# One encoder layer for two groups: the queries' rotation by one product and transfers inside SBUF

## The chip, the cores and the metric

One core of one Trainium2 chip. The metric is the device time of one execution in microseconds; lower is better. Five engines work beside each other, each with its own queue that runs in order: TensorE (PE; its weight loads are shown as PEld), VectorE (DVE), ScalarE (ACT), GpSimd (POOL) and SyncE (SP), which issues most transfers. 16 DMA engines move the data.

## The reference, cut to what matters

One layer of a bidirectional encoder is applied to two groups ("prompt" and "sample") of 512 tokens, 1024 channels, with shared weights: norm, an input projection, an mLSTM branch and a latent attention branch, gates that merge them, an output projection, a SwiGLU block, a gated embedding, a last norm. The change is in the attention branch, in the rotation of the queries:

```python
def rope(x, cos, sin):
    x1, x2 = jnp.split(x, 2, axis=-1)
    return jnp.concatenate([x1 * cos - x2 * sin, x1 * sin + x2 * cos], axis=-1)

qa = (rmsnorm(c_q, g_q) @ w_uq).reshape(B, S, A_HEADS, A_NOPE + A_ROPE)
q_nope = qa[..., :A_NOPE]                       # 128 channels
q_rope = rope(qa[..., A_NOPE:], cos, sin)       # 64 channels, x1 and x2 of 32 each
k_rope = rope(k_r, cos, sin)                    # one key of 64 channels for all heads
s = q_nope @ k_nope.T + q_rope @ k_rope.T       # for each of 8 heads
p = softmax(s * scale)
o = p @ v
```

## The kernel before, in words

Activations lie transposed, channels on the 128 partitions and the 512 tokens of a group along the free axis, so a tile is 128x512 in fp32. Matmuls get about fp32 precision from three products of operands split into a high and a low part (ScalarE casts the high part, VectorE subtracts it from the source to get the low one).

The stages in order: input projections and mLSTM; some merge gates (`merge_gate`: a projection by TensorE, a product by VectorE, a tanh, a store through a tile of the tag "bk"); the values of all heads, stored to DRAM through tiles of the tags "ch" and "bk" in turn (lines 703 and 704, 16 tiles `av`); attention; then the merge, the output projection, the SwiGLU block and the rest as long chains of matmuls.

Attention runs over 8 heads, and for each over the 2 groups g. `attn_proj(hd, g)` prepares head hd: for even heads it makes the rotated queries of two heads at once (2 x 64 = 128 rows), then the query and key tiles (`qn`, `kn`), and loads the head's values (`avt`). All three projections go through one PSUM bank, tag "pj", of which there is one. `attn(hd, g)` makes the scores in four blocks, softmax, transposes and the product with the values; its output `oz` is copied into a tile of the tag "ch" and stored. In the program, head hd+1's projections of a group follow head hd's attention of that group.

`rope(src, nblk)` (lines 711 to 722) rotates nblk blocks of 32 rows. For the queries nblk is 4 and `src` is the bank "pj"; it is called 8 times, for heads 0, 2, 4, 6 and two groups. These are called the first to the eighth rotation here; they begin at 568.1, 581.3, 643.9, 669.3, 723.9, 747.1, 791.9 and 809.4 us. For the key nblk is 2. Line 714 makes the product with the cosines for all rows. Line 718 makes the product with the sines block by block and writes each to its neighbour block's rows of a scratch tile `rs` (blocks 0 and 1 change places, 2 and 3 too; the sign is in the table). Line 721 adds. Scratch `rs`, result `rp` and the loaded values `avt` share the tag "tr", which has three buffers. Behind the rotation, lines 744 to 747 split the result into high and low parts for the two heads.

Two things set the order around the change. A tile pool gives out the buffers of a tag in turn, in the order of the program, and a tile's first writer waits until the last user of the buffer's tile before is done, a store's transfer among them; the tag "ch" has two buffers. And the order on each engine's queue is not the program's: a planner simulates the kernel with its own durations and lays each queue out by the times at which it finds the instructions ready. Only stretches marked as pinned keep the program's order; the attention stage is not among them.

Of the kernel before, what the change touches and what calls it, by code (L numbers as in the profile page):

```python
# [11 lines left out]
ALU = mybir.AluOpType  # L12
# [50 lines left out]
def encoder_kernel(ctx: ExitStack, tc: tile.TileContext, a):  # L63
    nc = tc.nc
# [20 lines left out]
    V, S, E, GP = (Engine(e) for e in (nc.vector, nc.scalar, nc.tensor, nc.gpsimd))  # L85
# [23 lines left out]
    EV = Slots("EV", ch=2, bk=2)  # L109
# [249 lines left out]
    for g in range(G):  # L359
        s = EV("ch", "gsb")  # L360
# [25 lines left out]
    for d in range(2):  # L386
        st = R("tr", "mst")
        nc.sync.dma_start(st[:, 0:P], a["mask"][d])
        m = MC.pool.tile([P, P], F32R, name=f"mask{d}")
# [50 lines left out]
    for i in range(NB):  # L440
        c = slice(i * P, (i + 1) * P)
        V.tensor_tensor_scan(
            out=M[:, c], data0=A[0][:, c], data1=A[0][:, c], initial=mprev[:, i : i + 1], op0=ALU.max, op1=ALU.max
# [4 lines left out]
    for d in range(1, NB):  # L448
        GP.tensor_copy(out=A[d][:, (NB - d) * P : T], in_=A[0][:, (NB - d) * P : T])
        for j in range(NB - d):  # L450
            e = (j + d) * P - 1
            V.tensor_scalar(
                out=A[d][:, j * P : (j + 1) * P],
                in0=A[d - 1][:, j * P : (j + 1) * P],
# [12 lines left out]
    for d in range(NB + 1):  # L467
        src = A[d] if d < NB else em
# [239 lines left out]
    sin = Q.pool.tile([P, T], F32, name="sin")  # L708
    nc.sync.dma_start(sin, a["sin"])

    def rope(src, nblk):
        n = 32 * nblk
        r = Q("tr", "rp")
        V.tensor_tensor(out=r[0:n], in0=src[0:n], in1=cos[0:n], op=ALU.mult)
        s = Q("tr", "rs")
        for i in range(nblk):
            o = i ^ 1
            V.tensor_tensor(
                out=s[32 * o : 32 * o + 32], in0=src[32 * i : 32 * i + 32], in1=sin[32 * i : 32 * i + 32], op=ALU.mult
            )  # L720
        V.tensor_tensor(out=r[0:n], in0=r[0:n], in1=s[0:n], op=ALU.add)
        return r

    kst = []
    for g in range(G):
        gs = Q("tr", "gs")
        nc.sync.dma_start(gs[0:64], gsd[g])
        r = rope(gs, 2)
        kh = Q.pool.tile([P, T], F32R, name=f"kh{g}")
        kl = Q.pool.tile([P, T], F32R, name=f"kl{g}")  # L730
        for o in (0, 64):
            S.copy(kh[o : o + 64], r[0:64])
        for o in (0, 64):
            V.tensor_tensor(out=kl[o : o + 64], in0=r[0:64], in1=kh[0:64].bitcast(F32), op=ALU.subtract)
        kst.append((kh, kl))
# [3 lines left out]
    def attn_proj(hd, g, wa):  # L739
        if hd % 2 == 0:  # L740
            r = rope(proj1(wa, lat["cq"][g], 2, 0, "pj"), 4)
            st0 = Q("qst", "qs0", F32R)
            st1 = Q("qst", "qs1", F32R)
            S.copy(st0[0:64], r[0:64])
            S.copy(st1[64:128], r[64:128])
            V.tensor_tensor(out=st0[64:128], in0=r[0:64], in1=st0[0:64].bitcast(F32), op=ALU.subtract)
            V.tensor_tensor(out=st1[0:64], in0=r[64:128], in1=st1[64:128].bitcast(F32), op=ALU.subtract)
            qst[g] = [st0, st1]
        qn = split(proj1(wa, lat["cq"][g], 2, 256, "pj"), Q, "qkv", "qn")
        kn = split(proj1(wa, lat["ckv"][g], 2, 512, "pj"), Q, "qkv", "kn")  # L750
        vt = Q("tr", "avt")
        c = hd % 4 * P
        nc.sync.dma_start(vt.rearrange("p (a b) -> p a b", a=NB), vd[g][hd // 4].rearrange("a p c -> p a c")[:, :, c : c + P])
        vn = split(vt, Q, "qkv", "vn", GP)
        return qn, kn, vn, qst[g][hd % 2]
# [699 lines left out]
```

## Time and profile before

| | |
|---|---|
| time, median of 3 runs | 1897.68 us (1896.53 to 1899.62) |
| profiled execution | 1901.48 us, of which the span 1899.3 us |
| TensorE busy | 1849.6 us, 97% |
| VectorE busy | 1232.7 us, 65% |
| ScalarE busy | 881.6 us, 46% |
| GpSimd busy | 457.4 us, 24% |
| mean granted TensorE clock | 0.991 |

The span runs from the first to the last instruction of the profiled execution. Matmuls are pipelined and the profile models their ends, so a busy TensorE is one that has work under way, not one at its peak. Line numbers (L718) are those of the kernel before; a line can be that of a helper. "PEclk" is the clock that TensorE was granted, as a share of 2.4 GHz.

### The profile page before, as it was taken

The numbers are of one execution on the slowest core, as the hardware profiler recorded it, in microseconds if no ns is written. First come the engines' busy times: TensorE is split into PE (matmuls) and PEld (weight loads), VectorE is DVE, ScalarE is ACT, GpSimd is POOL, SyncE is SP. The second block draws the span as 40 slices with busy tenths as digits, with TensorE's granted clock in tenths as the row PEclk, the third lists the DMA queues.
The fourth block names the chain that finished last, engine by engine and source line by source line (L and its number), as shares of the span: only waits on it lengthen the run. The fifth ranks groups of instructions, "written<-read, shape, count | busy, mean of one in ns | idle before, by whom it ended". The sixth has DMA issues, their size and how long they took to land.

```text
span 1899.3 us, 24534 instructions
## 1 busy us (share of the span) xinstructions
PE 1849.6 (97%) x8849; PEld 1536.6 (81%) x8849; DVE 1232.7 (65%) x2158; ACT 881.6 (46%) x1717; POOL 457.4 (24%) x326
## 2 busy tenths in 40 slices
PE   9999999999999998999999998999999999999997
PEld 6888898988888877777877887888888887887886
DVE  6747575836555567885897586444444458878757
ACT  6255555534444565774534354333333344433432
POOL 1000000100000000332350035666466643322100
PEclk9999999999999999999999999999999999999998
DMA  4111111112253124345555241232323346534232
GB/s 164 51 45 35 56 34 66 36 56 73 84 187 121 53 70 119 95 150 197 164 189 185 94 164 56 89 133 92 103 90 111 112 148 226 164 127 135 88 122 89
DMA packets 98314, 207.60 MB, mean 109 GB/s; under 512 B 10704, under 2 KB 21328, under 8 KB 98192
## 3 DMA queue, kind: packets, MB, share of 16 engines
q1 hardware_dynamic: 86096, 163.03, 25.8%
q10 hardware_dynamic: 12096, 43.00, 7.0%
q8 instruction: 70, 1.15, 0.2%
q14 instruction: 52, 0.43, 0.1%
HBM read 151.89 MB, written 54.10 MB: 108 GB/s over the span
## 4 chain that ended last, share of the span: by engine, by line
PE 84%; DVE 10%; ACT 2%; DMA 2%; issue 2%; SPq 0%; DVEq 0%; ACTq 0%
PE b L917 12%; PE b L919 12%; PE b L918 12%; PE mm L183 8%; PE mm L185 8%; PE mm L184 8%; PE mm L79 3%; PE nm L603 3%; DVE xl L154 2%; PE mm L518 2%; PE mm L520 2%; PE mm L519 2%; DVE wp L154 1%; PE mm L1265 1%; PE mm L1266 1%
## 5 line engine op out<-in xcount | busy, mean ns | idle before, releaser
L919 PE MATMUL b<-xh,wp 128*128 128x512 f32 x1148 | 445.1, 393 | 7.4 <-DVE wp L154 7.4
L917 PE MATMUL b<-xh,wp 128*128 128x512 f32 x1148 | 442.3, 394 | 10.0 <-ACT wp L866 4.5
L918 PE MATMUL b<-xl,wp 128*128 128x512 f32 x1148 | 448.9, 392 | 0.0
L866 ACT CAST wp<-wst 128x512 fp32r<-128x512 f32 (+1 forms) x270 | 164.2, 612 | 309.9 <-PE b L919 264.4
L154 DVE TENSOR_TENSOR wp<-wst,wp 128x512 fp32r<-128x512 f32 (+1 forms) x270 | 240.8, 893 | 76.5 <-ACT wp L866 76.0
L917 PEld LDWEIGHTS b<-xh,wp 128*128 128x128 f32 x1148 | 216.6, 189 | 63.6 <-ACT wp L866 9.1
L919 PEld LDWEIGHTS b<-xh,wp 128*128 128x128 f32 x1148 | 216.4, 188 | 55.9 <-DVE wp L154 8.8
L918 PEld LDWEIGHTS b<-xl,wp 128*128 128x128 f32 x1148 | 216.3, 188 | 46.6
L183 PE MATMUL mm<-hh,whi 128*128 128x512 f32 x560 | 219.4, 392 | 0.0
L184 PE MATMUL mm<-hl,whi 128*128 128x512 f32 x560 | 219.3, 392 | 0.0
L185 PE MATMUL mm<-hh,wlo 128*128 128x512 f32 x560 | 218.9, 393 | 0.0
L892 POOL TENSOR_TENSOR s<-wst,wst 128x512 f32<-128x512 f32 (+1 forms) x42 | 67.2, 1600 | 425.0 <-DMA wst<-w 270.1
L957 DVE TENSOR_TENSOR u<-b,u 128x512 f32<-128x512 f32 x90 | 61.6, 689 | 143.8 <-PE b L919 87.4
L183 PEld LDWEIGHTS mm<-hh,whi 128*128 128x128 f32 x560 | 105.6, 188 | 22.0 <-DVE va L526 0.3
L184 PEld LDWEIGHTS mm<-hl,whi 128*128 128x128 f32 x560 | 105.6, 189 | 21.8
L185 PEld LDWEIGHTS mm<-hh,wlo 128*128 128x128 f32 x560 | 105.5, 188 | 21.8
L168 ACT CAST whi<-wst 128x1024 fp32r<-128x1024 f32 (+1 forms) x69 | 71.0, 1028 | 104.3 <-PE mm L184 61.8
L952 ACT COPY u<-b 128x512 f32<-128x512 f32 x90 | 50.9, 589 | 107.4 <-PE b L919 80.0
L154 DVE TENSOR_TENSOR xl<-ld,xh 128x512 fp32r<-128x512 f32 x121 | 92.3, 793 | 12.3 <-ACT xh L1199 6.5
L154 DVE TENSOR_TENSOR wlo<-wst,whi 128x1024 fp32r<-128x1024 f32 (+1 forms) x69 | 83.6, 1212 | 23.2 <-ACT whi L168 23.0
L154 POOL TENSOR_TENSOR vnl<-avt,vnh 128x512 fp32r<-128x512 f32 x16 | 21.4, 1339 | 306.2 <-ACT vnh L158 283.5
L895 POOL TENSOR_TENSOR wst<-wst,wst 128x512 f32<-128x512 f32 (+1 forms) x42 | 79.1, 1884 | 38.0 <-DVE wp L154 28.6
(348 smaller groups left out, 3632.7 us busy)
## 6 DMA issues: line engine op xcount, KB each, us to landing
wst<-w SPq DMA_DIRECT2D x74, 512.0 KB
wst<-w ACTq DMA_DIRECT2D x60, 512.0 KB
ld<-actd SPq DMA_DIRECT2D x77, 256.0 KB
actd<-t SPq DMA_DIRECT2D x44, 256.0 KB
actd<-sg SPq DMA_DIRECT2D x33, 256.0 KB
x<-x SPq DMA_DIRECT2D x32, 256.0 KB
ld<-hzd SPq DMA_DIRECT2D x32, 256.0 KB
wst<-wd ACTq DMA_DIRECT2D x16, 512.0 KB
```

The costliest lines, as they stand in the source:

```text
L154: e.tensor_tensor(out=out, in0=src, in1=hi.bitcast(F32), op=ALU.subtract)
L168: S.copy(hi[:, :n], st[:, :n])
L183: E.matmul(bk, whi[:, c], hi, start=k == 0, stop=False)
L184: E.matmul(bk, whi[:, c], lo, start=False, stop=False)
L185: last_mm[0] = E.matmul(bk, wlo[:, c], hi, start=False, stop=k == nk - 1)
L866: S.copy(hi, src)
L892: GP.tensor_tensor(out=src, in0=a11, in1=a21, op=ALU.add)
L895: GP.tensor_tensor(out=a11, in0=a11, in1=a21, op=ALU.add)
L917: E.matmul(bk, whi[:, c], hi, start=bool(first) and k == 0, stop=False, **sk)
L918: E.matmul(bk, whi[:, c], lo, start=False, stop=False, **sk)
L919: E.matmul(bk, wlo[:, c], hi, start=False, stop=k == self.kh - 1, **sk)
L957: V.tensor_tensor(out=t, in0=b, in1=t, op=ALU.add if name == "P2" else ALU.subtract)
```

## The change

For the rotations of four blocks, the products with the sines become one product of all 128 rows into a new tile `rm` of the tag "ch", and four transfers on SyncE's queue, each of 32 rows (64 KB), copy its blocks into the neighbour block's rows of the scratch tile. The addition that follows is as before. The key's rotation (two blocks) is as before.

```diff
         s = Q("tr", "rs")
+        m = EV("ch", "rm") if nblk == 4 else None
+        if m is not None:
+            V.tensor_tensor(out=m, in0=src, in1=sin, op=ALU.mult)
         for i in range(nblk):
-            o = i ^ 1
-            V.tensor_tensor(
-                out=s[32 * o : 32 * o + 32], in0=src[32 * i : 32 * i + 32], in1=sin[32 * i : 32 * i + 32], op=ALU.mult
-            )
+            f, o = slice(32 * i, 32 * i + 32), slice(32 * (i ^ 1), 32 * (i ^ 1) + 32)
+            if m is not None:
+                nc.sync.dma_start(s[o], m[f])
+            else:
+                V.tensor_tensor(out=s[o], in0=src[f], in1=sin[f], op=ALU.mult)
         V.tensor_tensor(out=r[0:n], in0=r[0:n], in1=s[0:n], op=ALU.add)
```

## Rows read from the trace of the kernel before

**Rows 1.** The page: span and busy time of each engine.

```profile
span 1899.3 us, 24534 instructions
...
PE 1849.6 (97%) x8849; PEld 1536.6 (81%) x8849; DVE 1232.7 (65%) x2158; ACT 881.6 (46%) x1717; POOL 457.4 (24%) x326
```

**Rows 2.** Busy time by stretch; its first line names the columns.

```profile
core 0: us, PE busy (x) PEld busy (x) DVE busy (x) ACT busy (x) POOL busy (x), PEclk, DMA share, GB/s
565.00:600.00 35.00, 35.00 (x160) 29.00 (x159) 22.96 (x36) 17.25 (x31) 2.24 (x2) 1.00 0.45 147
640.00:680.00 40.00, 38.34 (x182) 30.70 (x181) 29.62 (x63) 24.53 (x50) 2.58 (x2) 1.00 0.23 75
...
720.00:760.00 40.00, 34.33 (x156) 27.35 (x155) 32.99 (x65) 24.78 (x50) 2.69 (x3) 0.94 0.40 114
760.00:800.00 40.00, 36.74 (x177) 28.95 (x175) 36.76 (x73) 31.72 (x67) 13.56 (x10) 0.97 0.37 113
800.00:835.00 35.00, 33.09 (x160) 26.82 (x161) 26.75 (x60) 25.03 (x53) 5.13 (x4) 1.00 0.12 38
```

**Rows 3.** The chain of waits, 640 to 835 us: shares by line.

```profile
by line: PE pt L782 6.3%; PE mm L183 5.5%; PE mm L184 5.4%; PE mm L185 5.4%; PE pj L183 4.9%; DVE rs L718 4.7%; PE pj L184 4.5%; PE pj L185 4.5%; PE av L789 4.0%; PE av L790 3.9%; PE av L791 3.9%; DMA ld<-hzd 3.7%; PE sc L765 3.4%; PE sc L7
```

**Rows 4.** Line 718: count, min/median/max ns, first and last start.

```profile
L718 DVE TENSOR_TENSOR rs<-pj,sin x32: 680/686/697, 568.8 to 812.2; 32x512 f32<-32x512 f32 x32
```

**Rows 5.** Line 714, the same view: all 128 rows.

```profile
L714 DVE TENSOR_TENSOR rp<-pj,cos x8: 667/681/692, 568.1 to 809.4; 128x512 f32<-128x512 f32 x8
```

**Rows 6.** TensorE's waits, 560 to 835 us: total us, times, longest.

```profile
PE pj L183 <- DVE rs L718: 2.8, 2, 1.7
```

**Rows 7.** VectorE in time order, fourth rotation: start, us, instruction.

```profile
670.01 2.79 DVE L718 TENSOR_TENSOR rs<-pj,sin 32x512 f32<-32x512 f32 x4
...
675.56 0.68 DVE L721 TENSOR_TENSOR rp<-rp,rs 128x512 f32<-128x512 f32 x1
```

**Rows 8.** VectorE in time order, sixth, seventh and eighth rotation.

```profile
747.83 2.79 DVE L718 TENSOR_TENSOR rs<-pj,sin 32x512 f32<-32x512 f32 x4
...
754.25 0.69 DVE L721 TENSOR_TENSOR rp<-rp,rs 128x512 f32<-128x512 f32 x1
...
792.56 2.79 DVE L718 TENSOR_TENSOR rs<-pj,sin 32x512 f32<-32x512 f32 x4
...
796.18 0.68 DVE L721 TENSOR_TENSOR rp<-rp,rs 128x512 f32<-128x512 f32 x1
...
810.06 2.79 DVE L718 TENSOR_TENSOR rs<-pj,sin 32x512 f32<-32x512 f32 x4
...
814.88 0.68 DVE L721 TENSOR_TENSOR rp<-rp,rs 128x512 f32<-128x512 f32 x1
```

**Rows 9.** SyncE's queue in time order: small transfers issued early on.

```profile
51.46 0.36 SPq L400 DMA_DIRECT2D lf<-rid  x1
...
60.49 0.62 SPq L420 DMA_DIRECT2D rfn<-lfd  x2
```

**Rows 10.** VectorE: the first instruction behind each [idle before it].

```profile
53.25 0.23 DVE L401 SCALAR_TENSOR_TENSOR u<-lf 128x64 f32<-128x64 f32 x1 [4.10 <-DMA lf<-rid]
...
63.77 0.42 DVE L423 COPY rf<-rfn 32x512 f32<-32x512 f32 x1 [3.73 <-DMA rfn<-lfd]
```

**Rows 11.** Load of the key's rows: SyncE's queue, then VectorE.

```profile
541.95 0.46 SPq L727 DMA_DIRECT2D gs<-gsd  x1
...
546.67 0.68 DVE L714 TENSOR_TENSOR rp<-gs,cos 64x512 f32<-64x512 f32 x1 [0.99 <-DMA gs<-gsd]
```

**Rows 12.** SyncE's queue: stores of value tiles.

```profile
555.67 2.48 SPq L704 DMA_DIRECT2D vd<-av  x3
...
572.84 0.32 SPq L704 DMA_DIRECT2D vd<-av  x1
```

**Rows 13.** ScalarE in time order: the fifth value tile is written.

```profile
560.19 0.59 ACT L703 COPY av<-mm 128x512 f32<-128x512 f32 x1 [0.98 <-DMA vd<-av]
```

**Rows 14.** The chain of waits, 740 to 815 us, one of the longest pieces.

```profile
737.51 2.61 DMA tad<-tg
```

## The prediction

> **What bounds the kernel now.** I read the page first, then busy time by stretch, then the chain of waits over the stage that holds the rotations, then the single rotations in order of time. On the page TensorE is busy for 97% of the span [rows 1]; a change to VectorE can pay only where TensorE stands idle for it, so the question is which stretch that is. The eight rotations of queries begin between 568 and 809 us [rows 5]. By stretch [rows 2], TensorE is busy for the whole of 565 to 600 us, where the first two lie. From 640 to 680 it loses 1.7 us, from 720 to 760 5.7, from 760 to 800 3.3, from 800 to 835 1.9. In those same stretches VectorE is busy 74%, 82%, 92% and 76% of the time, and from 760 to 800 ScalarE, at 79%, is the next. So the late part of attention is set by VectorE and the early part by TensorE. The chain of waits agrees: of 640 to 835 us, line 718 (the sine products) has 4.7%, which is 9.2 us, the largest share of any VectorE line that the row shows [rows 3]. Six rotations lie in that span, with 6 x 2.79 = 16.7 us of sine products; a little over half of it is on the chain. TensorE waits twice, 2.8 us in all, straight for the sine product that releases its single pj bank [rows 6].
>
> **The change part by part.**
>
> *Three products go.* A product of 32 rows takes 686 ns [rows 4], one of all 128 rows out of the same bank 681 ns [rows 5]. Four become one: 3 x 0.69 = 2.07 us of VectorE less per rotation, 16.6 us in eight. What is on the path: the first and second lie where TensorE is dense [rows 2], and I count them at nothing; so I do with the third and fifth, as the 9.2 us of sine products on the chain are no more than some three to four rotations of 2.79. The work that hides these four is TensorE's own dense sequence. If that cover were gone each would give up to 2.07. The fourth, sixth, seventh and eighth (products at 670.0, 747.8, 792.6 and 810.1 us [rows 7, 8]) lie in stretches bound by VectorE: 4 x 2.07 = 8.3 us. The 2.8 us of waits for the bank are within this, as the bank comes free 2.07 us sooner.
>
> *Four transfers come.* They wait for the product, and the addition (line 721) waits for them on VectorE's queue, which runs in order; whatever is queued behind the addition waits too, and ScalarE's casts and TensorE's transposes for that. No row shows a transfer from SBUF to SBUF. The nearest: two small loads issued together at 60.49 us let VectorE go on at 63.77, 3.3 us later; one, issued at 51.46, at 53.25, 1.8 us later [rows 9, 10]. With other traffic about, the 128 KB of the key rows took from 541.95 to 546.67, 4.7 us [rows 11], and a value tile's store, issued at 555.67, held the next writer of its buffer until 560.19, 4.5 us [rows 12, 13]. An issue costs 0.31 us (two in 0.62), so the fourth goes out 0.93 us after the first. The rows therefore put the scratch between 0.93 + 1.8 = 2.7 and 0.93 + 4.7 = 5.6 us behind the product; the pair is the row most like it, and with two more issues gives 3.3 + 0.62 = 3.9 us, which I take.
>
> What covers 3.9 us? Between the end of the first product and the addition there were 4.9, 5.7, 2.9 and 4.1 us in the four rotations that count [rows 7, 8]; without the three products 2.8, 3.7, 0.9 and 2.1 us of other VectorE work are left, 9.4 in all. With this work alone the additions would stand for 1.1 + 0.2 + 3.0 + 1.8 = 6.1 us (3.9 less each), and of the 8.3 us only 2.2 would be left. But the order of the queue is written anew, and the planner puts other instructions ahead of one that waits for a transfer. How well it does this is shown by the key rows: its plan left 0.99 us of idle time behind the transfer [rows 11]. I take 1.0 us per rotation, 4.0 us, and keep 6.1 for the range. The queries' own way to the scores gets some 2 us longer; I cost that at nothing after the first head, as the rotation of two heads on is issued well ahead of its scores; if that lead is gone, it is 2 us per rotation.
>
> *SyncE.* 32 issues x 0.31 = 9.9 us of a queue that mostly waits. Behind a transfer that waits for its product stand loads of value tiles, weights and stores. I take nothing; the bound is one rotation's four issues, 1.2 us, for each of the four loads behind them that VectorE or ScalarE waits for, 5 us.
>
> *Buffers.* The product goes to the two-buffer "ch" tag, and that is new. The first rotation's product takes the buffer of the thirteenth value tile, whose store is issued at 572.84 [rows 12]; at 2.6 us (a store on the chain [rows 14]) to 4.5 us [rows 13] it is free at 575.4 to 577.3, 6.6 to 8.5 us after the sine products began at 568.8 [rows 4]. The pj bank is held for as long, and with it the head's two other projections. TensorE has the rest of the values and the merge gates to run, so I take 1.0 us, with bounds of 0 and 8.5. Later products wait for the store of an attention output; in the seventh rotation that store comes a few microseconds after the place where the product is now, and I cost the slide at nothing, with a bound of 3. The three-buffer scratch tag holds its tile 2 us longer; a value tile's load behind it starts later, hidden by a head's length.
>
> *Clock.* From 720 to 760 us the granted clock is 0.94 [rows 2], behind the gaps around the sixth rotation: 0.06 x 40 = 2.4 us. A shorter gap may keep it at 2.4 GHz; I take a third, 0.8 us, between 0 and 2.4.
>
> *Sum.* -8.3 + 4.0 + 1.0 - 0.8 = -4.1 us. The profiled execution took 1901.48 us (span 1899.3 and 2.2 around it) and would take 1897.4; the median of the runs shown, 1897.68, is 3.8 us or 0.2% below it, and the forecast for it is 1893.6 us.
>
> **The rivals.** *Nothing to measure.* The additions stand for 6.1 us instead of 4.0 and the clock is not won, -8.3 + 6.1 + 1.0 = -1.2: 1896.5 us. For it: TensorE's idle time is small and shared with ScalarE, which needs its own time in 760 to 800 us. Against: TensorE's waits name line 718 itself [rows 6].
>
> *Slower: the addition at the head of VectorE's queue.* Place: the same four rotations. If the scratch comes 5.6 us behind the product, as the key rows' load would make it [rows 11], the other work covers 9.4 of 22.4 us, the additions stand for 13.0 us, and the sum is -8.3 + 13.0 + 1.0 = +5.7: 1903.4 us. It decides from (9.4 + 8.3) / 4 = 4.4 us behind the product, the point at which the stall eats the products. For it: 40% of the transfer engines' time is in use at 720 to 760 us and 37% at 760 to 800, against 12% in the last stretch [rows 2]. Against: the 4.5 us and 4.7 us come from stretches with more traffic (45% at 565 to 600), and the planner knows of the wait. The Trainium skill, "DMA: Bandwidth & Descriptors", section "Queues, rings and completion order", speaks for this rival: all transfers that one engine issues share a row of rings, and each transfer engine takes its descriptors there in order, so the exchange would queue behind a bulk load issued before it. The rows of 4.5 and 4.7 us agree with that but do not prove it.
>
> *The change does not act as written: a new order.* The planner, given other durations, lays out the whole stage anew; the products then land beside other waits, and the first rotation's buffer (bound 8.5 us) may cost more than 1.0. Its sign is open: I put it at -3 to +6 us, 1894.7 to 1903.7.
>
> **How the numbers follow.** Forecast 0.40; nothing to measure 0.28; the addition 0.17; a new order 0.15. A change of 0.2%, 3.8 us, is about what a measurement of this kernel can tell from none. The forecast lies just beyond that: of its 0.40, 0.28 falls faster and 0.12 same; of the second, 0.05 faster, 0.21 same, 0.02 slower; of the third, 0.14 slower and 0.03 same; of the last, 0.05, 0.04 and 0.06. That makes 0.38 faster, 0.40 same, 0.22 slower. The range: the best end is 8.3 + 2.4 = 10.7 us less, 1887.0 us; at the other end the third case's 1903.4. Both ends are bounds of a cost and the tails beyond them about 0.1 each. The forecast's own range is 1889 to 1896.
>
> **What would show it.** Line 718 leaves the 128-row rotations and becomes one product of about 0.68 us, eight of them; VectorE's busy time falls by about 16.6 us. Right, if TensorE's idle time from 640 to 835 us falls by several microseconds, and VectorE's idle time put down to the exchange stays near 1 us a rotation. Wrong, if it waits 3 us or more before line 721, or if TensorE shows gaps before 640 us, where it had none. It would also be wrong if the gain came with the first rotations, which I count at nothing.

## The result, and the profile after

The changed kernel takes 1904.05 us (median of 8 runs, 1901.34 to 1905.25) against 1898.24 for the kernel before beside it (8 runs): a ratio of 1.0024, 95% interval 1.0015 to 1.0033, so it is slower by 3 to 6 us. Forecast were 1893.6 us; the sign was wrong and the time lies just above the range's end of 1903.4.

The work did change as written. The page after (answering to [rows 1]), and lines 718 and 722 by instruction (count, min/median/max ns, first and last start; [rows 4]):

```profile
span 1903.1 us, 24569 instructions
...
PE 1854.3 (97%) x8849; PEld 1539.1 (81%) x8849; DVE 1215.5 (64%) x2134; ACT 882.2 (46%) x1717; POOL 458.7 (24%) x326
```

```profile
L718 DVE TENSOR_TENSOR rm<-pj,sin x8: 672/682/693, 575.0 to 817.2; 128x512 f32<-128x512 f32 x8
```

```profile
L722 SPq DMA_DIRECT2D rs<-rm x32: 507/582/591, 575.7 to 819.7; - x32
```

VectorE lost 17.2 us of work (16.6 forecast), and the span still grew by 3.8 us. Busy time by stretch after, columns as in [rows 2]:

```profile
565.00:600.00 35.00, 34.63 (x153) 28.30 (x152) 14.22 (x24) 14.28 (x25) 1.29 (x1) 1.00 0.49 162
640.00:680.00 40.00, 37.73 (x181) 30.53 (x180) 24.06 (x51) 23.17 (x46) 2.59 (x2) 1.00 0.19 63
...
720.00:760.00 40.00, 36.31 (x171) 28.84 (x170) 23.59 (x48) 21.97 (x43) 3.67 (x3) 0.98 0.37 110
760.00:800.00 40.00, 37.04 (x164) 28.29 (x162) 35.46 (x72) 32.68 (x68) 12.92 (x10) 0.93 0.44 134
800.00:835.00 35.00, 31.13 (x135) 24.33 (x136) 24.88 (x52) 22.21 (x46) 5.23 (x4) 0.90 0.23 68
```

From 565 to 600 us TensorE now loses 0.4 us where it lost nothing, which the prediction named as a sign of being wrong. From 640 to 835 us it loses 14.7 us instead of 12.5, and from 800 to 835 us alone 3.9 instead of 1.9, at a mean clock of 0.90 instead of 1.00. VectorE is less busy than before in each of these stretches: it is waited for, but not because it is full. VectorE's waits from 560 to 880 us (total us, times, longest) name what for:

```profile
DVE rm L718 <- DMA vd<-av: 7.1, 1, 7.1
...
DVE rp L725 <- DMA rs<-rm: 2.7, 3, 1.5
```

The additions wait 2.7 us for the exchange, in all eight rotations together. The new product waits 7.1 us for a store of a value tile, once. The product is late in other rotations too, but there VectorE does not stand idle for it: the planner put other work ahead of it. In the seventh rotation, VectorE in order of time:

```profile
795.80 0.67 DVE L714 TENSOR_TENSOR rp<-pj,cos 128x512 f32<-128x512 f32 x1
...
806.33 0.67 DVE L718 TENSOR_TENSOR rm<-pj,sin 128x512 f32<-128x512 f32 x1
```

and TensorE's last matmul into the bank pj before that, and the next one:

```profile
794.04 0.39 PE L185 MATMUL pj<-cqh,wlo 128*128 128x512 f32 x1
...
807.34 0.47 PE L183 MATMUL pj<-cqh,whi 128*128 128x512 f32 x1
```

The two products read the same bank. Before, the sine products followed at once; now the second product starts 10.5 us after the first, and the only pj bank takes no projection for 13 us (4.6 us before). From the first to the second product's start, the eight rotations have 7.7, 0.6, 11.8, 4.1, 10.5, 0.6, 10.5 and 0.6 us; where nothing stands between, it is 0.6. In the seventh the buffer in ch is that of an attention output whose store SyncE issued at 798.38 us:

```profile
798.38 0.32 SPq L798 DMA_DIRECT2D ozd<-oz  x1
```

By the trace's semaphores that store was complete at 800.37 us, 6 us before the product started. In the fifth rotation it is plainer. The store of the buffer's tile before was issued ahead of the first product and complete at 723.41 us, 12 us before the second:

```profile
721.25 0.32 SPq L798 DMA_DIRECT2D ozd<-oz  x1
```

```profile
725.22 0.69 DVE L714 TENSOR_TENSOR rp<-pj,cos 128x512 f32<-128x512 f32 x1 [1.71 <-PE pj L185]
...
735.69 0.67 DVE L718 TENSOR_TENSOR rm<-pj,sin 128x512 f32<-128x512 f32 x1
```

In the fourth, too, the buffer was free before the first product. In the third and seventh it came free 1.9 and 3.9 us after the first product's end, and the second still started 9 and 6 us later. So only in the first rotation does VectorE stand waiting for the buffer. In the other four most of the gap, or all of it, is the product's place in VectorE's queue, which the planner gave it when the tile came from ch. Why the planner chose so late a place is not shown.

What follows is the projections of head 6 being late. ScalarE copies the last attention output of head 5 at 814.82 us, 6 us earlier than before (820.87), and then has none of head 6 until 840.92, 5 us later than before (835.88):

```profile
814.82 0.59 ACT L797 COPY oz<-av 128x512 f32<-128x512 f32 x1 [0.38 <-ACT vnh L158]
```

```profile
840.92 0.58 ACT L797 COPY oz<-av 128x512 f32<-128x512 f32 x1
```

Between the two TensorE waits 2.4 us for a key tile and then runs at the lower of its two levels, matmuls 0.43 us apart (0.23 at 2.4 GHz):

```profile
827.41 1.47 PE L769 MATMUL sc<-knh,qnh 128*128 128x512 f32 x2 [2.41 <-ACT knh L158]
828.68 0.63 PE L183 MATMUL pj<-cqh,whi 128*128 128x512 f32 x1
829.11 0.63 PE L184 MATMUL pj<-cql,whi 128*128 128x512 f32 x1
```

The last attention output is copied at 872.59 us, 6.6 us later than before (865.99). So the loss is made in attention; 2.8 us of it come back behind it.

### The profile page after: what moved, and what is told of

Same layout as the page of the kernel before. It is cut to its first block, busy times and chain, and to the rows that moved or that the text cites. A ratio compares the mean times of both kernels' runs of the same rounds, so it can differ in the third digit from the quotient of the medians.

```text
span 1903.1 us, 24569 instructions
## 1 busy us (share of the span) xinstructions
PE 1854.3 (97%) x8849; PEld 1539.1 (81%) x8849; DVE 1215.5 (64%) x2134; ACT 882.2 (46%) x1717; POOL 458.7 (24%) x326
## 4 chain that ended last, share of the span: by engine, by line
PE 85%; DVE 8%; ACT 3%; issue 2%; DMA 2%; SPq 0%; POOL 0%; DVEq 0%; ACTq 0%; POOLq 0%
PE b L921 12%; PE b L923 12%; PE b L922 12%; PE mm L183 8%; PE mm L185 8%; PE mm L184 8%; PE mm L79 3%; PE nm L603 3%; DVE xl L154 2%; PE mm L518 2%; PE mm L520 2%; PE mm L519 2%; DVE wp L154 1%; PE mm L1270 1%; PE mm L1269 1%
```

## The experiments

Each was timed in turns with the kernel before on the same chip. The groups of kernels ran on different chips, so kernels are compared by their ratios to the kernel before. Changes in us are a ratio's difference from 1 times 1899.

**Is it the buffer or the transfers?** Four kernels. The first takes the product's buffer from the tag s3, which nothing else uses until the merge:

```diff
-        m = EV("ch", "rm") if nblk == 4 else None
+        m = WX("s3", "rm") if nblk == 4 else None
```

> The changed kernel with one difference: the 128-row product is written to a buffer of the tag s3 (two buffers that nothing else uses before the merge), not of ch. Transfers as changed. Theory BUFFER (the product waits for a ch buffer and holds the only pj bank meanwhile; that is the loss): the product follows the cosine product within about 1 us in all eight rotations, and the time is 1893 to 1898, at or below before. Theory TRANSFER (the addition and what is behind it wait for the four transfers): as changed, 1902 to 1906. Theory LAYOUT (any edit makes the planner lay the stage out anew, and the time moves by a few us either way): 1894 to 1905, without a pattern over the four runs.

Measured: 1884.49 us against 1899.96, ratio 0.9920 (0.9907 to 0.9934): 15 us *faster* than before, beyond what any theory gave. The gap between the two products is 0.6 us in all eight rotations; the seventh:

```profile
784.70 0.69 DVE L714 TENSOR_TENSOR rp<-pj,cos 128x512 f32<-128x512 f32 x1
785.30 0.68 DVE L718 TENSOR_TENSOR rm<-pj,sin 128x512 f32<-128x512 f32 x1
```

and in these two stretches TensorE loses nothing and 0.7 us, at full clock:

```profile
640.00:680.00 40.00, 40.00 (x193) 32.96 (x192) 26.70 (x60) 25.14 (x52) 2.58 (x2) 1.00 0.29 92
...
800.00:835.00 35.00, 34.28 (x174) 28.56 (x173) 28.60 (x64) 27.79 (x59) 12.14 (x10) 1.00 0.39 128
```

The second keeps the kernel before, four products and no transfers, and only moves the scratch to ch:

```diff
-        s = Q("tr", "rs")
+        s = EV("ch", "rs") if nblk == 4 else Q("tr", "rs")
```

> The kernel before, its four 32-row products kept and no transfers, but for the queries' rotations the scratch tile comes from the tag ch in place of tr. BUFFER: slower than before, 1901 to 1906, with the first sine product of several rotations some us behind the cosine product. TRANSFER: as before, 1896 to 1900. LAYOUT: 1894 to 1905.

Measured: 1915.19, ratio 1.0086 (1.0072 to 1.0100), 16 us slower with no transfer at all. The third rotation:

```profile
654.24 0.68 DVE L714 TENSOR_TENSOR rp<-pj,cos 128x512 f32<-128x512 f32 x1
...
668.03 2.79 DVE L718 TENSOR_TENSOR rs<-pj,sin 32x512 f32<-32x512 f32 x4
```

The third and fourth have one product and no transfers; the addition reads the product, without the exchange:

```diff
+        if nblk == 4:                          # s from "tr"; in the other kernel from "ch"
+            V.tensor_tensor(out=s, in0=src, in1=sin, op=ALU.mult)
```

> One 128-row product straight into the scratch tile of tr, no transfers, nothing from ch; the exchange of the blocks is left out of the computation. It shows what the three products are worth alone. BUFFER and TRANSFER both: 1889 to 1894 (the 8.3 us that the prediction put on the path, less what ScalarE keeps). LAYOUT: 1894 to 1905.

Measured: 1893.40, ratio 0.9968 (0.9957 to 0.9979), 6 us faster.

> One 128-row product into a tile of ch, which the addition reads directly: the coupling to ch without the transfers; the exchange is left out of the computation. BUFFER: 4 us or more slower than the product alone in tr, 1896 to 1903. TRANSFER: as the product alone, 1889 to 1894. LAYOUT: 1894 to 1905.

Measured: 1909.91, ratio 1.0051 (1.0038 to 1.0063), 10 us slower. TRANSFER is refuted by three of the four. BUFFER has the sign right in all four, but its ranges were too narrow in three: each moved further than it said. The same three lie outside the range of LAYOUT.

**Was a wait for tr in the kernel before too, and which place loses?**

```diff
-        s = Q("tr", "rs")                       # the kernel before, four products
+        s = WX("s3", "rs") if nblk == 4 else Q("tr", "rs")
```

> The kernel before with its four products and no transfers; only the queries' scratch tile comes from s3 in place of tr. Theory BUFFER, widened (a wait for any scratch buffer, tr's in the kernel before too, holds the pj bank): faster than before by 4 to 10 us, 1888 to 1895. Theory SAVED WORK (what the changed kernel with a free buffer gained, 15 us, is the three products): as before, 1896 to 1901.

Measured: 1898.04, ratio 0.9984 (0.9975 to 0.9993): 3 us, as SAVED WORK had it. The tag tr was hardly a wait; the widened theory falls.

The same with one product, no transfers and no exchange:

> One 128-row product into a tile of s3 that the addition reads directly; no transfers, the exchange is left out of the computation. Against the changed kernel with a free buffer (1884.5) it differs by the transfers alone. Transfers hidden: 1882 to 1887. Transfers cost (additions held): 1876 to 1881. If the gap between the product alone in tr (1893.4) and this one is small, the tr buffer was no wait: 1890 to 1894.

Measured: 1894.29, ratio 0.9973 (0.9962 to 0.9985). That is about the product alone in tr (0.9968), so tr was no wait here either. The transfers cost nothing: with them it is 1884.49 (0.9920). No theory had expected that.

```diff
+        m = EV("ch", "rm") if rot[0] < 2 else WX("s3", "rm")     # the other kernel: rot[0] >= 2
```

> The changed kernel with the first and second rotation's product in ch, the other six in s3. If the loss sits at the value tiles' stores in front of the first rotation: 1895 to 1904. If it sits at the attention outputs' stores later: 1884 to 1889.

Measured: 1891.22, ratio 0.9957 (0.9943 to 0.9970); only the first rotation's gap is long (7.8 us). The time lies between the two ranges.

> The changed kernel with the first and second rotation's product in s3, the other six in ch. If the loss sits at the value tiles' stores: 1884 to 1889. If it sits at the attention outputs' stores: 1895 to 1904. Both places share it if this run and the one with ch for the first two each lose 5 to 12 us.

Measured: 1903.43, ratio 1.0019 (1.0010 to 1.0028); the gaps of the third, fourth, fifth and seventh are 19.6, 4.0, 10.5 and 8.8 us. Against the kernel with all eight in s3, ch costs 7 us at the first two rotations and 19 us at the last six. The two do not add up: with all eight in ch it is 20 us.

**Why do transfers gain with a free buffer?** 1884.49 with (0.9920), 1894.29 without (0.9973).

```diff
-                nc.sync.dma_start(s[o], m[f])
+                GP.tensor_copy(out=s[o], in_=m[f])
```

> The changed kernel with the product in s3 and the exchange by four 32-row copies on GpSimd instead of four transfers. The transfers seem to have gained 9 us (1884.5 with them, 1894.3 without). Theory DELAY (an addition that must wait is put behind the softmax work of the heads in front, which is needed sooner; any delay of some us does it): 1882 to 1889. Theory DMA (something that only transfers bring, such as SyncE's queue being shifted): 1892 to 1897.

Measured: 1892.37, ratio 0.9967 (0.9955 to 0.9980), in the range of DMA.

```diff
-        (four transfers of 32 rows)
+            nc.sync.dma_start(s, m)             # product in s3; no exchange
```

> The changed kernel with the product in s3 and one transfer of all 128 rows in place of four; the exchange is left out of the computation. DELAY: 1882 to 1889. DMA: also near 1884 if a transfer as such matters, 1888 to 1893 if the four issues and their place in SyncE's queue do. LAYOUT (a small difference makes another plan): anywhere from 1884 to 1895.

Measured: 1884.64, ratio 0.9926 (0.9913 to 0.9940), as with four. The four issues are not what gains.

```diff
+        s = WX("s3", "rm")                      # four products as before, into s
+        nc.sync.dma_start(t, s)                 # then one transfer to the tr scratch
```

> The kernel before with its four products, written to s3, and one transfer of all 128 rows from there to the tr scratch that does nothing but delay the addition. With no products saved, DELAY expects 1886 to 1893 (faster than the four products in s3, 1898.0). SAVED WORK expects 1897 to 1902, at or above it. LAYOUT: 1890 to 1902.

Measured: 1897.58, ratio 0.9991 (0.9983 to 1.0000): a transfer as a pure delay gains nothing with four products. DELAY misses here and with GpSimd. Against the kernel with one product and one transfer (0.9926), which differs by the three products alone, it is 12 us slower: the transfers gain only together with the saved products.

The traces showed another difference: VectorE's wait for the loads ld<-hzd that the merge needs. Its totals from 560 to 880 us, in the kernel before, the free buffer with transfers and without:

```profile
DVE ld L828 <- DMA ld<-hzd: 3.5, 2, 2.5
```

```profile
DVE ld L832 <- DMA ld<-hzd: 0.6, 1, 0.6
```

```profile
DVE ld L829 <- DMA ld<-hzd: 4.3, 2, 2.7
```

Four kernels try whether this is the rest. Transfers on ScalarE's queue:

```diff
-                nc.sync.dma_start(s[o], m[f])
+                S.dma_start(s[o], m[f])
```

> The changed kernel with the product in s3, its four transfers issued from ScalarE's queue, so that SyncE's queue carries nothing new. Theory DELAY (the waiting addition itself gains): 1882 to 1889. Theory HOP (the gain beyond the product alone, 9 us, is VectorE not waiting for the loads for the merge, ld<-hzd, around 740 us, a matter of where the new plan puts them): 1884 if VectorE's wait for ld<-hzd stays under 1.5 us, 1890 to 1896 if it is 3 to 5 us again.

Measured: 1892.17, ratio 0.9963 (0.9951 to 0.9976), with 2.5 us of wait for ld<-hzd, between the two cases named, and 9.0 us for the transfers.

No transfers, and the loads off SyncE's queue, to ScalarE's and to GpSimd's:

```diff
-        return load(hzd[g][k], *stage[raws[0] % 4])
+        S.dma_start(t, hzd[g][k])               # the other kernel: GP.dma_start
```

> One 128-row product in s3, no transfers (exchange left out of the computation), and the loads ld<-hzd made during attention issued from ScalarE's queue, no longer behind stores on SyncE's. HOP: VectorE's wait for them falls from 4.3 us to under 1.5 and the time from 1894.3 to 1884 to 1890. DELAY: 1891 to 1897.

Measured: 1890.50, ratio 0.9950 (0.9936 to 0.9963). The wait fell from 4.3 us:

```profile
DVE ld L829 <- DMA ld<-hzd: 0.8, 1, 0.8
```

> As the run before it, the loads issued from GpSimd's queue. HOP: under 1.5 us of wait and 1884 to 1890. DELAY: 1891 to 1897. A third outcome, slower than 1897, would be the loads being served late from that queue.

Measured: 1889.18, ratio 0.9945 (0.9932 to 0.9957), and no such wait is left.

```diff
-        V.tensor_tensor(out=r[0:n], in0=r[0:n], in1=s[0:n], op=ALU.add)
+        (GP if nblk == 4 else V).tensor_tensor(out=r[0:n], in0=r[0:n], in1=s[0:n], op=ALU.add)
```

> The changed kernel with the product in s3 and the queries' addition on GpSimd, so that VectorE never waits for the transfers. DELAY: 1880 to 1888 (VectorE is freed of 0.7 us more per rotation). HOP: 1880 to 1888 with a wait for ld<-hzd under 1.5 us, 1888 to 1895 with 3 us or more.

Measured: 1889.09 (the middle of five runs; four lie between 1886.53 and 1890.00, one took 6541.56), ratio 0.9940 (0.9926 to 0.9953), with 0.4 us of wait for ld<-hzd: a little slower than HOP and DELAY gave. With VectorE freed of the addition and of its waits for the transfers, nothing was gained over the free buffer alone.

So moving these loads off SyncE's queue gains 4 to 5 of the 10 us. That this is by VectorE's wait for them, as HOP has it, is not shown: the kernel with GpSimd's copies has 1.2 us of that wait and takes 1892.37, and the one with four products and one transfer has 1.4 us and takes 1897.58. What makes the rest stays open: it came with transfers from SyncE's queue, one or four, and not with GpSimd's copies, ScalarE's queue or four products. LAYOUT, a plan that happens to be better, fits this and is only argued.

## Why the prediction was wrong

The step that failed is *Buffers*. It saw that the product goes to ch, that the first rotation waits for a value store (6.6 to 8.5 us forecast; 7.1 us of wait measured), that later products wait for an attention output's store, and that the pj bank is held meanwhile. It then took 1.0 us for all this, with the seventh rotation's slide "at nothing, with a bound of 3". Measured, ch costs 19 us with four products (ratios 1.0086 and 0.9984), 15 without transfers (1.0051, 0.9973) and 20 with them (1.0024, 0.9920). The gap was 10.5 us in the seventh rotation and 4 to 12 in the third, fourth and fifth, which the prediction does not price. For the "nothing" it gives no reason. The mistake in reasoning: it priced the tile by the moment at which a store is done. In these four rotations the buffer was free 6 to 12 us before the product started, and what held the product from then on was the new order of VectorE's queue. All the while the bank was held through which the query and key tiles of the same head must pass. That the loss comes by way of that bank is read from the trace; no run gave pj a second bank. The prediction also took the values and the merge gates, which keep TensorE dense, as cover. They only ran earlier and were missing later: TensorE had 135 matmuls into the bank mm from 560 to 600 us, before 118, and 96 from 640 to 720 us, before 110; in that second stretch it lost 4.1 us, before 1.7.

*Three products go* had the sign right and a size that is no constant: 8.3 us were put on the path, and one product against four gains 6 us in tr (0.9968), 7 in ch (1.0051 against 1.0086), 2 in s3 (0.9973 against 0.9984) and 12 in s3 with one transfer in each kernel (0.9926 against 0.9991). That the early rotations give nothing was not tested.

*Four transfers come* was right in kind, and its wait too dear. Issues cost 0.58 us, not 0.31. By the trace's semaphores each transfer landed 1.9 to 2.8 us after its issue, and the last of four 3.3 to 6.0 us behind the product (3.9 forecast). But the additions waited 2.7 us in all and not 4.0, and that in the first, second and fifth rotation, not in the four that were counted; with the free buffer they waited 4.9 us. No pair of kernels shows a cost of the transfers: 1.0024 against 1.0051 in ch, 0.9920 against 0.9973 in s3. The traffic beside the two rows that the prediction priced by, 4.5 and 4.7 us, it read from another stretch (45% at 565 to 600 us); from 541 to 548 and from 555 to 561 us, where they lie, it was 75% and 87%. The slower rival, the addition at the head of VectorE's queue behind slow transfers, is refuted as the cause. Its reason, the ring order of the Trainium skill's "DMA: Bandwidth & Descriptors" (section "Queues, rings and completion order"), is neither refuted nor shown: the changed kernel's transfers landed within 2.8 us of their issue, while the slowest with the free buffer took 4.4, and no run tells what it met.

*Clock* came true in its place and was lost again behind it: the granted clock rose from 0.94 to 0.98 from 720 to 760 us, and fell from 0.97 to 0.93 from 760 to 800 and from 1.00 to 0.90 from 800 to 835 us.

The rival "a new order" was the nearest: it named the first rotation's buffer and a range of 1894.7 to 1903.7, with a chance of 0.15. The time, 1904.05, lies just above that range. The loss is that of the tag ch, mostly at the last six rotations, and there by the new order rather than by the store.

## What to carry to other kernels

A new tile in a shared tag ties its writer to whatever held that buffer last, on the chip and in the order that a planner lays out. Price it not by the moment at which the buffer comes free but by what its writer holds until its turn comes, here the only PSUM bank of a whole stage. Such a hold need not show as idle time of the writer's engine; here it shows as the gap between two readers of one bank. The same edit with a buffer that nobody else uses is 15 us faster than before instead of 5 slower: 1884.5 us, the best version here. With a planner that lays queues out anew, try the edit in pairs (each tag with and without the other part) before believing a difference of a few microseconds: here two kernels that differ by the exchange transfers and the tile that they write lay 10 us apart, and the one with the transfers was the faster.

## What the runs showed that was not expected

A transfer of 32 rows between two SBUF tiles holds SyncE's queue for 0.58 us, a store of 128 rows to DRAM for 0.32. Taking 17 us of VectorE's work away, or adding thirty-two transfers, moved the time less than which of two tags a scratch tile came from.
